# GLA decay differences as masked products on TensorE, moved gate stores and another issue plan in a hybrid SSD / GLA / RWKV-7 layer stack

## The chip, the cores and the metric

One core of a Trainium2 chip runs the whole program in a single launch. TensorE (PE) multiplies, with its weight loads listed apart as PEld; VectorE (DVE), ScalarE (ACT) and GpSimd (POOL) work element by element; SyncE (SP) issues most DMAs. The metric is the device time of one execution in microseconds, the median of several runs. The PE's clock has two levels, 1.2 and 2.4 GHz; the profile gives the share granted.

## The reference

Two layers (`DEPTH` 2) run over 128 context tokens and 256 latent tokens of width 1024. Each layer has a SwiGLU block, a token mixer of three scan branches (Mamba-2 SSD, GLA, RWKV-7, each forward and backward) and a second SwiGLU block. The change touches the GLA branch, which is, with chunks of C = 64 tokens:

```
lg = log_sigmoid(lr @ gk_w[d] + gk_b[d]) / 16
bc = cumsum(lg, within a chunk)
diff = bc[:, :, :, None] - bc[:, :, None, :]
decay = exp(where(causal, diff, -inf))
A = einsum('bnthk,bnshk,bntshk->bnhts', q, k, decay)
o_intra = einsum('bnhts,bnshv->bnthv', A, v)
q_dec = q * exp(bc);  k_dec = k * exp(last - bc)
S_{n+1} = exp(last) * S_n + k_dec^T v;  o = o_intra + q_dec @ S_n
```

There are 4 heads of 64 key and 128 value channels, and both directions are summed before an RMS norm, a gate and an output product.

## The kernel before

**Layout.** Activations stand with channels on the 128 partitions and all T = 384 tokens (6 chunks of 64) in the free dimension. The four GLA heads are two pairs (`hp` 0 and 1), each filling 128 partitions. Dense products are split in high and low fp32r parts: three products each, weights `wh` and `wl` made by ACT (`wh`) and DVE (`wl`) from a loaded tile `wraw`.

**The mixer's order.** The mixer first projects, and puts aside in DRAM, what the branches need; the last of this are the gates of three branches (`gates`, L1083 and on): a dense product in `psd`, a tanh on ACT into one of two staging tiles `sa`, and a store issued by SP. After the RWKV scan, `rwkv_out` of its second half and `gla_decays` (L1733) run together, with the last gate projections (`mhh`, `mhl`) as dense work between. Then `scans` (L811) runs the GLA lanes, the SSD lanes and the RWKV branch's output product (`ob` with `w_rw_o`, 96 dense products) together, and at the end the output products of GLA and SSD and the common output projection.

**What sets the order.** All lanes are Python generators. `pace` calls them in turn; while no lane is due, it issues single dense products. A lane says when it is due by the model `Clock` (L105): each instruction is put on its engine at an estimated time (`place`), and `yield` hands back when its operands are estimated to be there. So a change of the model's costs or rules moves instructions. Each engine then runs its own list in order and waits by semaphores. Because mixer instructions pass through the wrapper `Timed`, nearly all of them carry line L275 in the profile; the tile names tell them apart.

**GLA decays.** `gla_decays` forms for each pair and direction the gate `log_sigmoid` (tiles `gde` on ACT, `gdm` on DVE, table loads between exponential and logarithm), and its running sum within chunks by a scan on DVE: tile `b`, one for each pair and direction.

**GLA levels.** `gla_levels` (L1834) never forms the 64 x 64 x 64 decay. It cuts a chunk in six levels of halves; at each, with `b` of the middle token m, q takes exp(b_t - b_m) and k takes exp(b_m - b_s). For a pair and level, DVE takes two differences and POOL two (`gD<-b`), ACT one exponential of 768 columns (`gD<-gD`), DVE multiplies the half for q and POOL the half for k (`gD<-gD,glqk`), PE forms 12 products of 64 x 64, and DVE takes the level's entries into `A` by a masked copy (`gA`, COPY_PREDICATED). The operands of one level are made ahead.

**GLA states and output.** `gla_states` (L1777) makes exp(b) (`qe`) and exp(last - b) (`ke`) by DVE and ACT, q and k times these (`qd` on POOL, `ke` on DVE), and carries the states (`gS`). `gla_output` adds all products, then takes the norm (`gn`) and the gate (`go`, with `ggs`). The second pair's states wait for the first pair's output. The SSD stages beside it use `sR`, `sE`, `sD`, `sct`, `sx`.

Of the kernel before, what the change touches and what calls it, by code (L numbers as in the profile page):

```python
# [92 lines left out]

def split_evenly(n, parts, i):

    return n * (i + 1) // parts - n * i // parts if i < parts else 0
# [15 lines left out]
class Clock:  # L112
# [9 lines left out]

    LAG = dict(tensor=196, scalar=135, vector=128, gpsimd=75)
    LAG_TO = dict(tensor=50, gpsimd=30)

    def __init__(self, nc):
        self.nc = nc
        self.done = 0.0
# [12 lines left out]
    def place(self, engine, t, cost):  # L141
# [157 lines left out]
class GlaPair:  # L299


    def __init__(self):
        self.vt = self.A = None
        self.qd, self.states, self.done = {}, {}, False
# [33 lines left out]
class Kernel:  # L338
# [415 lines left out]
    def mixer_(self, l, nxt):  # L754
# [7 lines left out]
        with ExitStack() as st:  # L762
# [4 lines left out]
            with pool("mh") as mh, pool("stg") as self.stg, pool("rwp") as rp:  # L767
# [25 lines left out]
                decays = {}  # L793
# [17 lines left out]
    def scans(self, l, gp, sp, obp, decays, gin, sin, j):  # L811

        I = self.I
        go, lanes, pairs = self.gla(l, gp, decays, *gin[1:])
# [269 lines left out]
    def gates(self, l, b):  # L1084
# [616 lines left out]
    def gla(self, l, gp, b, q, k, v):  # L1701

        nc = self.nc
        o = gp.tile([128, 4, T], F32, name="go")
# [8 lines left out]
        def states(d):  # L1713
            for hp in range(2):
                p = P[hp]
                if d == 0:
                    p.vt = yield from self.gla_values(gp, v[:, 2 * hp:2 * hp + 2, :])
                yield from wait(lambda: p.vt is not None and (hp == 0 or P[0].done))
                yield from self.gla_states(l, gp, hp, d, q[:, hp, :], k[:, hp, :], b[hp, d], p)
# [4 lines left out]
        def levels():  # L1724
            for hp in range(2):
                P[hp].A = yield from self.gla_levels(gp, q[:, hp, :], k[:, hp, :], b[hp, 0], b[hp, 1])
                P[hp].gs = gp.tile([128, 2, T], F32, tag="gD", bufs=3, name="ggs")
# [5 lines left out]
    def gla_decays(self, l, gp, tp, b):  # L1733
        nc = self.nc
        gk = tp.tile([128, 2, 256], F32, name="gk")
        nc.gpsimd.memset(gk[64:96], 0.0)
# [3 lines left out]
        for hp in range(2):  # L1740
            em = []
            for d in range(2):
                bias = self.pa[l][:, A_GKB + 2 * d + hp:A_GKB + 2 * d + hp + 1]
                ps = self.psm()[:, :T]
                nc.tensor.matmul(ps, gk[64:96, d, 128 * hp:128 * hp + 128], self.misc[64:96, :], start=True, stop=True)
                e = tp.tile([128, T], F32, tag="te", bufs=2, name="gde")
# [474 lines left out]
```

## Time and profile before

| | us |
|---|---|
| median of 3 runs | 2452.38 |
| lowest and highest run | 2447.63, 2454.55 |
| profiled execution | 2450.24 |
| its span | 2448.2 |
| PE busy | 2308.2 |
| DVE busy | 1760.1 |
| ACT busy | 1104.5 |
| POOL busy | 510.1 |

The profile comes from one execution. Its page gives busy times and groups of equal instructions, and the trace behind it answers questions on single instructions, on what an engine waited for, and on stretches of the span. A group's row reads: line, engine, operation, written tile <- read tiles, shapes, count | busy time of all, mean ns of one | idle time before them and what ended it. The scan part of the first layer lies at about 742 to 906 us of the span, that of the second at about 1930 to 2097.

### The profile page before, as it was taken

To read this page: it belongs to the slowest core of one execution; us is meant where nothing else is said; L and a number is where in the kernel's file an instruction comes from. 1 tells how busy PE (TensorE), PEld (TensorE's weight loads), DVE (VectorE), ACT (ScalarE), POOL (GpSimd) and SP (SyncE) were. 2 spreads that over 40 slices of the span, in tenths; PEclk is the share of its full clock that TensorE was granted. 3 is DMA by queue.
4 is the path that set the end of the run, shared out by engine and by line. 5 is a ranking of instruction groups with operands and counts; after the bars stand their busy time and mean duration, and the time that the engine had idled before them with its cause. 6 is when DMAs were issued, how large, how long until landed. Compare 5 with 4: busy or idle time off the path is not lost. (4 is left out here: it accounts for less than half of the span.)

```text
span 2448.2 us, 48785 instructions
## 1 busy us (share of the span) xinstructions
PE 2308.2 (94%) x19825; PEld 2132.0 (87%) x19825; DVE 1760.1 (72%) x3152; ACT 1104.5 (45%) x2009; POOL 510.1 (21%) x582
## 2 busy tenths in 40 slices
PE   6999899899999879999999999989999987899998
PEld 4999897888877669999999999878888766899998
DVE  3968769776658987878486877995767597785433
ACT  3533346354435455543345334743544544463322
POOL 3100024212215641100120001441212275120000
PEclk7999999999999999999999999989999998999999
DMA  9766554334425226567465766423443431554432
GB/s 305 234 206 208 175 157 109 90 94 130 115 63 156 68 84 209 170 195 214 132 189 170 226 207 170 134 77 103 109 110 102 125 103 31 177 181 131 128 118 81
DMA packets 501663, 354.14 MB, mean 145 GB/s; under 512 B 40035, under 2 KB 479985, under 8 KB 500927
## 3 DMA queue, kind: packets, MB, share of 16 engines
q1 hardware_dynamic: 496288, 337.44, 46.9%
q0 software_dynamic: 3680, 6.18, 1.2%
q10 hardware_dynamic: 1471, 7.41, 0.8%
q8 instruction: 155, 2.54, 0.4%
q14 instruction: 69, 0.57, 0.1%
HBM read 326.59 MB, written 24.38 MB: 143 GB/s over the span
## 5 line engine op out<-in xcount | busy, mean ns | idle before, releaser
L649 ACT CAST wh<-wraw 128x1024 fp32r<-128x1024 f32 (+2 forms) x296 | 280.1, 956 | 585.7 <-issue 332.5
L650 DVE TENSOR_TENSOR wl<-wraw,wh 128x1024 fp32r<-128x1024 f32 (+2 forms) x296 | 330.8, 1125 | 220.6 <-ACT wh L649 220.3
L662 PE MATMUL psm<-xh,wl 128*128 128x384 f32 (+1 forms) x896 | 304.3, 340 | 5.8 <-DVE wl L650 5.8
L660 PE MATMUL psm<-xh,wh 128*128 128x384 f32 (+1 forms) x896 | 306.0, 342 | 0.6 <-DVE xh L608 0.6
L661 PE MATMUL psm<-xl,wh 128*128 128x384 f32 (+1 forms) x896 | 304.0, 339 | 0.0
L275 PE MATMUL psd<-mhl,wh 128*128 128x384 f32 x848 | 298.6, 352 | 2.6 <-DVE mhl L275 2.6
L275 PE MATMUL psd<-mhh,wh 128*128 128x384 f32 x848 | 295.2, 349 | 5.8 <-DVE sb L275 3.4
L275 DVE TENSOR_TENSOR wl<-wraw,wh 128x512 fp32r<-128x512 f32 x324 | 236.4, 742 | 85.4 <-ACT wh L275 78.7
L275 PE MATMUL psd<-mhh,wl 128*128 128x384 f32 x848 | 297.6, 351 | 0.0
L275 ACT CAST wh<-wraw 128x512 fp32r<-128x512 f32 x324 | 190.8, 614 | 174.3 <-PE psd L275 119.3
L536 DVE SCALAR_TENSOR_TENSOR aacc<-wada,cs,aacc 128x1024 f32<-128x1024 f32 x210 | 260.8, 1279 | 6.0 <-DMA wada<-in_w_ada_dram 5.6
L662 PE MATMUL psd<-gh,wl 128*128 128x384 f32 x704 | 237.1, 337 | 7.8 <-DVE wl L650 7.8
L660 PE MATMUL psd<-gh,wh 128*128 128x384 f32 x704 | 237.0, 337 | 0.0
L661 PE MATMUL psd<-gl,wh 128*128 128x384 f32 x704 | 236.5, 336 | 0.0
L621 POOL TENSOR_TENSOR acc<-acc,sq 128x384 f32<-128x384 f32 x24 | 28.9, 1205 | 718.6 <-ACT sq L619 709.2
L275 PEld LDWEIGHTS psd<-mhl,wh 128*128 128x128 f32 x848 | 162.6, 192 | 16.6 <-issue 8.1
L662 PEld LDWEIGHTS psm<-xh,wl 128*128 128x128 f32 x896 | 169.2, 189 | 8.1 <-DVE wl L650 7.9
L275 PEld LDWEIGHTS psd<-mhh,wh 128*128 128x128 f32 x848 | 162.7, 192 | 13.6 <-issue 5.8
L660 PEld LDWEIGHTS psm<-xh,wh 128*128 128x128 f32 x896 | 169.3, 189 | 6.0 <-issue 4.5
L660 PE MATMUL psm<-gh,wh 128*128 128x384 f32 x512 | 171.8, 336 | 0.0
L662 PE MATMUL psm<-gh,wl 128*128 128x384 f32 x512 | 171.1, 334 | 0.0
L661 PE MATMUL psm<-gl,wh 128*128 128x384 f32 x512 | 171.0, 334 | 0.0
(453 smaller groups left out, 4897.7 us busy)
## 6 DMA issues: line engine op xcount, KB each, us to landing
wada<-in_w_ada_dram SPq DMA_DIRECT2D x144, 512.0 KB, 4.8
wraw<-in_w_in_dram SPq DMA_DIRECT2D x112, 512.0 KB, 3.9
wraw<-in_ffn_gate_dram SPq DMA_DIRECT2D x88, 512.0 KB, 4.0
wraw<-in_ffn_up_dram SPq DMA_DIRECT2D x88, 512.0 KB, 4.7
wraw<-in_ffn_down_dram SPq DMA_DIRECT2D x64, 512.0 KB, 4.1
wraw<-in_ffn_down_dram SPq DMA_DIRECT2D x32, 384.0 KB, 4.6
gate<-sa SPq DMA_DIRECT2D x48, 192.0 KB, 2.3
gate<-gate SPq DMA_DIRECT2D x48, 192.0 KB, 2.5
```

Source lines behind the costliest of these rows:

```text
L275: r = f(*a, **k)
L536: nc.vector.scalar_tensor_tensor(out=acc[:, c], in0=w, scalar=x, in1=acc[:, c], op0=ALU.mult, op1=ALU.add)
L621: (nc.vector if k == KD - 1 else nc.gpsimd).tensor_tensor(out=self.acc, in0=self.acc, in1=sq, op=ALU.add)
L649: nc.scalar.copy(out=h[:, x], in_=r[:, x])
L650: nc.vector.tensor_sub(out=lo[:, x], in0=r[:, x], in1=h[:, x])
L660: nc.tensor.matmul(ps, wh, xh, start=first, stop=False)
L661: nc.tensor.matmul(ps, wh, xl, start=False, stop=False)
L662: nc.tensor.matmul(ps, wl, xh, start=False, stop=last)
```

## The change

Five things change together.

- `gla_decays` makes the gates with tokens on the partitions (12 products of 64 x 256 in place of 4 of 128 x 384, the bias from a loaded tile `gkb`), keeps the logarithms themselves, split in fp32r parts `lgh` and `lgl`, and makes no running sum.
- Every sum of logarithms that a level or a state needs is a product on PE with a column block of a 0/1 table `gsum` (128 x 1024, a new input built by `gla_sums`, loaded by POOL in each layer): `gla_sum` issues four products of 256 columns, and ACT takes the exponential straight from PSUM. This replaces the differences of DVE and POOL, `qe` and `ke` (now one tile `gE`).
- `gla_levels` goes through 9 stages for a pair (2 levels by 2 chunks each) in place of 6, with up to three operand tiles made ahead; a stage has one multiplication of 512 columns on DVE and one on POOL, 8 products of 64 x 64, and two masked copies of 128 columns.
- The stores of the last three gates of branch 0 are issued by POOL instead of SP.
- The model clock, during `scans`, puts an instruction in the first gap of its engine that holds it, with DVE, POOL and ACT costs taken 1.25, 1.3 and 1.1 times as long; before, it came behind all others of its engine. The output's gate tile `ggs` and the scratch of the norm get other places, and one SSD tile has three buffers for four.

```
@@ Clock @@
+    SLOWER = dict(vector=1.25, gpsimd=1.3, scalar=1.1)
...
-        if engine in ('vector', 'scalar', 'gpsimd'):
+        if self.gaps:
+            cost *= self.SLOWER.get(engine, 1.0)
+        elif engine in ('vector', 'scalar', 'gpsimd'):
@@ gates @@
-            self.nc.sync.dma_start(out=dst[i], in_=g)
+            (self.nc.gpsimd if b == 0 and i >= KD - 3 else self.nc.sync).dma_start(out=dst[i], in_=g)
@@ gla_sum, gla_inter: new @@
+        ps = self.psm()
+        for c in range(2):
+            for n, g in enumerate(b.parts):
+                nc.tensor.matmul(ps[:, 256 * c:256 * c + 256], g[:, 2 * j + c, 128 * hp:128 * hp + 128], b.sums[:, x:x + 256], start=(n == 0), stop=(n == 1))
+        nc.scalar.activation(out=out, in_=ps.rearrange("p (c s t) -> p c s t", c=2, s=4), func=AF.Exp, scale=1.0 / 16)
...
+        for j in range(3):
+            self.gla_sum(b, hp, j, 768, E[:, 2 * j:2 * j + 2])
...
+            nc.vector.tensor_mul(out=p.E[:, :, d, 1], in0=p.E[:, :, d, 1], in1=k)
...
+            nc.gpsimd.tensor_mul(out=p.E[:, :, d, 0], in0=p.E[:, :, d, 0], in1=q)
@@ gla_levels @@
-            nc.vector.tensor_tensor(out=DQ[:, :, 1], in0=f4[:, :, 1], in1=mf, op=ALU.subtract)
-            nc.vector.tensor_tensor(out=DQ[:, :, 0], in0=b4[:, :, 0], in1=mb, op=ALU.subtract)
-            nc.gpsimd.tensor_tensor(out=DK[:, :, 0], in0=mf, in1=f4[:, :, 0], op=ALU.subtract)
-            nc.gpsimd.tensor_tensor(out=DK[:, :, 1], in0=mb, in1=b4[:, :, 1], op=ALU.subtract)
-            nc.scalar.activation(out=DD, in_=DD, func=AF.Exp, scale=1.0 / 16)
-            nc.vector.tensor_mul(out=DD[:, 0], in0=DD[:, 0], in1=q)
-            nc.gpsimd.tensor_mul(out=DD[:, 1], in0=DD[:, 1], in1=k)
+            E = gp.tile([128, 2, 4, 64], F32, tag="gD", bufs=4, name="gD")
+            self.gla_sum(b, hp, j, 128 * lev, E)
+            E = E.rearrange("p c (l x) t -> p x c l t", l=2)
+            for i, eng in enumerate((nc.vector, nc.gpsimd)):
+                eng.tensor_mul(out=E[:, i], in0=E[:, i], in1=qk[i][:, 2 * j:2 * j + 2].unsqueeze(2).to_broadcast([128, 2, 2, 64]))
...
+            while len(nxt) < 3 and n + len(nxt) < len(stages):
+                nxt.append(operands(*stages[n + len(nxt)]))
```

How the lists of the engines move is shown at three places of the first layer. (In the changed kernel the wrapper's line is L300.)

POOL, from the end of the RWKV scan into the levels, before (`out_dram<-S` is the last RWKV state, `gk` the gate weights, `ro` the RWKV output, `dcol` and `ssi` are SSD's):

```order
L275 DMA out_dram<-S 128x2x64 x2
L275 MEMSET sC 128x768
L275 MEMSET gk 32x512
L275 DMA gk<-in_gla_gk_w_dram 16x256 x2
L275 TENSOR_TENSOR ro<-ro,kp 128x384 x2
L275 DMA dcol<-in_ssd_D_dram 64x4x1 x4
L275 DMA ssi<-in_state_ssd_dram 128x4x64 x2
L275 CAST smk<-kt 128x128 x3
```

and in the changed kernel:

```order
L300 DMA out_dram<-S 128x2x64 x2
L300 MEMSET sC 128x768
L300 DMA gsum<-in_sums_dram 128x1024
L300 MEMSET gk 64x512
L300 DMA gkb<-in_gla_gk_b_dram 64x256
L300 DMA gk<-in_gla_gk_w_dram 16x256 x2
L300 DMA gkb<-in_gla_gk_b_dram 64x256
L300 DMA gate_3181<-sa 128x384
L300 TENSOR_TENSOR ro<-ro,kp 128x384 x2
L300 DMA gate_3182<-sa 128x384
L300 DMA gate_3183<-sa 128x384
L300 DMA dcol<-in_ssd_D_dram 64x4x1 x4
```

The table load and a bias load stand ahead of the gate weights, and one gate store ahead of the `ro` product.

DVE, in the first pair's levels, before:

```order
L275 TENSOR_TENSOR gD<-b_8324 128x24x8
L275 TENSOR_TENSOR gD<-b_8328 128x24x8
L275 COPY_PREDICATED gA<-kt,psm 128x384
L275 TENSOR_TENSOR gD<-b_8324 128x48x4
L275 TENSOR_TENSOR gD<-b_8328 128x48x4
L275 SCALAR_TENSOR_TENSOR merged<-gate,psd 128x384
L275 TENSOR_TENSOR gD<-gD,glqk 128x384
```

and in the changed kernel:

```order
L300 TENSOR_TENSOR gD<-gD,glqk 128x4x64
L300 SCALAR_TENSOR_TENSOR merged<-gate,psd 128x384
L300 SCALAR_TENSOR_TENSOR gS<-gS,gtot,psm 128x128 x2
L300 COPY_PREDICATED gA<-kt,psm 128x128
L300 COPY gS<-psm 128x128
L300 COPY_PREDICATED gA<-kt,psm 128x128 x3
L300 SCALAR_TENSOR_TENSOR merged<-gate,psd 128x384
```

The differences are gone, and masked copies of a third of the size stand in their place.

PE, in the first pair's levels of the changed kernel; before, a level was one row `psm<-gD 64x64 x12` between dense products:

```order
L300 MATMUL psm<-gD 64x64 x8
L300 MATMUL psm<-gsum,lgh 128x256
L300 MATMUL psm<-gsum,lgl 128x256
L300 MATMUL psm<-gsum,lgh 128x256
L300 MATMUL psm<-gsum,lgl 128x256
L300 MATMUL psd<-ob,wh 128x384
L300 MATMUL psd<-ob,wl 128x384
```

The four sum products of a later stage follow the level products of the present one.

## Rows read from the trace of the kernel before

**Rows 1.** The page's part 1: busy time, share of the span and instructions.

```profile
PE 2308.2 (94%) x19825; PEld 2132.0 (87%) x19825; DVE 1760.1 (72%) x3152; ACT 1104.5 (45%) x2009; POOL 510.1 (21%) x582
```

**Rows 2.** Busy time by stretch; first layer's three stretches, second layer's levels.

```profile
core 0: us, PE busy (x) PEld busy (x) DVE busy (x) ACT busy (x) POOL busy (x), PEclk, DMA share, GB/s
742.00:763.00 21.00, 21.00 (x96) 16.19 (x94) 18.07 (x31) 18.95 (x30) 9.29 (x14) 1.00 0.55 133
763.00:834.00 71.00, 57.36 (x763) 48.53 (x764) 66.31 (x110) 32.94 (x63) 46.84 (x51) 0.92 0.40 114
834.00:906.00 72.00, 57.49 (x513) 46.28 (x509) 60.01 (x111) 36.77 (x74) 35.51 (x32) 0.92 0.16 48
...
1951.50:2022.00 70.50, 54.97 (x758) 46.48 (x759) 65.55 (x108) 32.26 (x61) 46.46 (x51) 0.94 0.40 113
```

**Rows 3.** Groups of instructions by form, both layers: level, state and POOL steps.

```profile
L275 POOL TENSOR_TENSOR gD<-gD,glqk 128x384 f32<-128x384 f32 x24 | 31.5, 1316 | 23.0 <-ACT gD L275 23.0
L275 DVE TENSOR_TENSOR gD<-b 128x192 f32<-128x192 f32 x48 | 27.9, 620 | 0.0
L275 DVE TENSOR_TENSOR gD<-gD,glqk 128x384 f32<-128x384 f32 x24 | 23.6, 984 | 3.8 <-ACT gD L275 3.8
L275 DVE COPY_PREDICATED gA<-kt,psm 128x384 f32<-128x384 int32 x24 | 13.9, 581 | 0.5 <-PE psm L275 0.4
L275 DVE SCALAR_TENSOR_TENSOR gS<-gS,qe,psm 128x128 f32<-128x128 f32 x32 | 9.6, 340 | 7.7 <-PE psm L275 5.1 <-DMA gS<-in_state_gla_dram 2.6
L275 DVE TENSOR_TENSOR ke<-ke,glqk 128x384 f32<-128x384 f32 x8 | 8.2, 1026 | 0.0
L275 DVE TENSOR_TENSOR ke<-b 128x384 f32<-128x384 f32 x8 | 7.1, 903 | 0.0
```

**Rows 4.** Timeline of DVE, two multiplications: start us, us, instruction, [idle before].

```profile
777.35 1.35 DVE L275 TENSOR_TENSOR gD<-gD,glqk 128x384 f32<-128x384 f32 x1
800.36 0.54 DVE L275 TENSOR_TENSOR gD<-gD,glqk 128x384 f32<-128x384 f32 x1
```

**Rows 5.** Timeline of POOL at the first of these.

```profile
776.98 1.31 POOL L275 TENSOR_TENSOR gD<-gD,glqk 128x384 f32<-128x384 f32 x1
```

**Rows 6.** Timeline of PE: gate products, two dense starts, one after small products.

```profile
750.80 1.55 PE L275 MATMUL psm<-misc,gk 32*128 32x384 f32 x4
...
754.14 0.34 PE L275 MATMUL psd<-mhh,wl 128*128 128x384 f32 x1
754.32 0.34 PE L275 MATMUL psd<-mhh,wh 128*128 128x384 f32 x1
...
794.75 0.44 PE L275 MATMUL psd<-ob,wh 128*128 128x384 f32 x1
```

**Rows 7.** Groups of ACT by form: exponentials from SBUF and from PSUM.

```profile
L275 ACT ACTIVATE gD<-gD 128x768 f32<-128x768 f32 x24 | 20.3, 846 | 32.0 <-DVE gD L275 25.3 <-POOL gD L275 6.7
L275 ACT ACTIVATE sct<-psm 128x512 f32<-128x512 f32 x16 | 9.1, 597 | 2.4 <-PE psm L275 2.4
```

**Rows 8.** Waits from 763 to 834 us: total us, times, longest us.

```profile
ACT gD L275 <- DVE gD L275: 12.5, 6, 3.2
...
PE psm L275 <- POOL gD L275: 4.2, 3, 2.9
...
ACT L275 <- DMA gate<-sa: 3.9, 1, 3.9
...
PE psd L275 <- ACT sa L275: 2.4, 1, 2.4
```

**Rows 9.** Timeline of POOL: issue of the gate weights.

```profile
738.81 1.03 POOL L275 DMA_DIRECT2D gk<-in_gla_gk_w_dram  x2 [0.29 <-POOL gk L275]
```

**Rows 10.** Groups of DVE by form, both layers: SSD and norm steps.

```profile
L275 DVE SCALAR_TENSOR_TENSOR sD<-scb,dt,sD 128x128 f32<-128x128 f32 x48 | 27.7, 608 | 1.8 <-ACT sD L275 1.8
L275 DVE TENSOR_TENSOR sE<-sE,sD 128x512 f32<-128x512 f32 x12 | 10.1, 840 | 0.1
L275 DVE SCALAR_TENSOR_TENSOR gn<-gn 128x384 f32<-128x384 f32 x8 | 8.0, 998 | 0.1
```

More of the change, by code (lines that the diff above doesn't have):

```diff
@@ L1703, in gla @@
         nc = self.nc
+        vt = [gp.tile([128, T // 64, 128], F32, tag="gvt", bufs=2, name="gvt") for hp in range(2)]
         o = gp.tile([128, 4, T], F32, name="go")
@@ L1762, in gla_values @@
-    def gla_values(self, gp, v):
-        nc = self.nc
-        NC = T // 64
-        vt = gp.tile([128, NC, 128], F32, tag="gvt", bufs=2, name="gvt")
+            nc.gpsimd.dma_start(out=bias[HS[d]], in_=self.I['gla_gk_b'][l, d].unsqueeze(0).to_broadcast([64, 256]))
+        em = []
+        for j in range(3):
+            ps = self.psm()
+            for c in range(2):
+                x = 64 * (2 * j + c)
+                for d in range(2):
+                    nc.tensor.matmul(ps[HS[d], 256 * c:256 * c + 256], self.misc[64:128, x:x + 64], gk[64:128, d, :], start=True, stop=True)
+            e, m = (tp.tile([128, 2, 256], F32, tag=n, bufs=3, name=n) for n in ("gde", "gdm"))
+            nc.vector.tensor_tensor(out=m, in0=ps.rearrange("p (c k) -> p c k", c=2), in1=bias.unsqueeze(1).to_broadcast([128, 2, 256]), op=ALU.add)
+            nc.scalar.activation(out=e, in_=m, func=AF.Abs)
+            nc.scalar.activation(out=e, in_=e, func=AF.Exp, scale=-1.0)
+            em.append((e, m))
+            yield self.soon()
@@ new lines, in gla_inter @@
+    def gla_inter(self, gp, hp, q, k, b, p):
+        nc = self.nc
+        E = gp.tile([128, 6, 4, 64], F32, tag="gE", bufs=1, name="gE")
+        for j in range(3):
+            self.gla_sum(b, hp, j, 768, E[:, 2 * j:2 * j + 2])
+            yield self.soon()
+        p.tot = gp.tile([128, 6, 2], F32, tag="gtot", bufs=2, name="gtot")
+        for d in range(2):
+            nc.scalar.copy(out=p.tot[:, :, d], in_=E[:, :, 2 * d, 63 if d == 0 else 0])
+        p.E = E.rearrange("p c (d x) t -> p c d x t", d=2)
+        q, k = (x.rearrange("p (c t) -> p c t", t=64) for x in (q, k))
+        for d in range(2):
+            nc.vector.tensor_mul(out=p.E[:, :, d, 1], in0=p.E[:, :, d, 1], in1=k)
+        p.ready = self.ck.done
+        for d in range(2):
+            nc.gpsimd.tensor_mul(out=p.E[:, :, d, 0], in0=p.E[:, :, d, 0], in1=q)
@@ new lines, in mask @@
+        def mask(lev, n):
+            return self.k(K_GM + 64 * lev, 64).unsqueeze(1).to_broadcast([128, n, 64])
+        nc.vector.tensor_tensor(out=A, in0=ps[:, 0:T].rearrange("p (c t) -> p c t", c=NC), in1=mask(6, NC), op=ALU.mult)
+        for n, (lev, j) in enumerate(stages):
+            while len(nxt) < 3 and n + len(nxt) < len(stages):
+                nxt.append(operands(*stages[n + len(nxt)]))
+                yield 0
+            E, t = nxt.popleft()
+            yield t
+            ps = self.psm()[:, 0:256].rearrange("p (l c t) -> p l c t", l=2, c=2)
+            for i in range(2):
+                for c in range(2):
+                    for hs in HS:
+                        nc.tensor.matmul(ps[hs, i, c], E[hs, 1, c, i], E[hs, 0, c, i], start=True, stop=True)
+            for i in range(2):
+                nc.vector.copy_predicated(out=A[:, 2 * j:2 * j + 2], mask=mask(lev + i, 2).bitcast(mybir.dt.int32), data=ps[:, i])
@@ L2038, in front @@
                 nc.tensor.matmul(pc[:, 0:256], Bm[:, bs], Cm[:, :, bs], start=True, stop=True)
-                cbs[b] = [sp.tile([128, 2, 128], F32, tag="scb", bufs=4, name="scb") for d in range(2)]
+                cbs[b] = [sp.tile([128, 2, 128], F32, tag="scb", bufs=3, name="scb") for d in range(2)]
                 for x, off in zip(cbs[b], (K_LE, K_GE)):
```

146 lines of the change are left out of this document (66 added, 80 removed).

## The prediction

> **What bounds the kernel now.** I read the page's busy times first: PE is busy for 94% of the span and DVE for 72% [rows 1], so over the whole program TensorE sets the time. But the change touches only the token mixer's scan part, once in each of the two layers, and an average over the program says nothing about that place. So I cut the first layer's scan part into three stretches and read the busy times of each [rows 2]: the decays (742 to 763 us), where PE is busy for all of 21 us; the level products (763 to 834), where DVE is busy for 66.3 of 71 us and PE for 57.4; and the tail (834 to 906: the second pair's states and outputs, and the SSD stages), where DVE has 60.0 and PE 57.5 of 72. The second layer's level stretch reads alike, 65.6 of 70.5 [rows 2], so everything below is worked out for one layer and doubled. In the decays every instruction added to PE is paid in full. In the level stretch VectorE is the bound, with a little over 13 us of idle PE beside it. The reader should see there how the waits run in a ring: the exponential on ACT and the products on PE wait for VectorE's and POOL's halves of the same operand tile [rows 8].
>
> **Decays.** Before, four fp32 products of 384 columns make the gates; two of them take 1.55 us with the last one's tail, so 0.75 each and 3.0 in all [rows 6]. Now there are twelve of 256 columns: at two thirds of 0.75 they take 6.0 us one after the other, and half of it, 3.0, if the two directions, which write different halves of the partitions, run side by side. So 0 to +3.0; I take +1.0, nearer to the lower end, since the small products of other lines run in such pairs already. POOL now loads the 512 KB mask table and one bias half ahead of the gate weights, which were issued at 738.81 for a first product at 742.18 [rows 9]. That product waits in PE's queue with the dense products behind it, so a late landing would be paid by PE: 0 to +2.5. The order puts 12 more dense products, 2.1 us at 0.173 [rows 6], ahead of the first gate product, and I take 0. VectorE's scans and two half-steps go and three wider steps and two splits come; the stretch is PE's, so they cost nothing while PE has its 58 dense products to run. POOL's queue gets the three gate stores, the first of them ahead of the `ro` product of the RWKV output, so this product waits for ACT's `sa`; it was needed only by the branch weights' first product after the dense ones, which is cover of about 8 us by the order. That they left SP frees the loads behind them; what this is worth stands in the next part. Decays: **+1.0**, between -0.5 and +5.
>
> **Levels, VectorE's work.** Per layer and in busy time (half of each row's sum, which covers both layers) there go 13.9 us of differences, 11.8 of multiplications, 6.9 of masked copies, and for the first pair 3.8 of the `ke` steps [rows 3]. In come 18 multiplications of 512 columns and 36 masked copies of 128. A multiplication of 384 columns takes 0.54 us at 800.36 but 1.35 at 777.35, where POOL was multiplying too [rows 4, 5], and 0.984 on average [rows 3]. Taken in proportion to the columns that is 0.72 to 1.31 on average; I take 1.1, nearer to the upper end, because one exponential still releases VectorE's and POOL's halves together: 19.8 us. A masked copy of 128 columns lies between a third of 0.581 and 0.581; the nearest row of that size is the `gS` step, which also reads PSUM, at 0.340 [rows 3]. I take 0.33: 11.9 us. The `gE` products of the first pair add two of 384 columns at about 0.8: 1.6. The order also moves work over the stretch's end: the first pair's normalisation (four `gn`, two `go`, one `ob`, about 0.8 each by [rows 10]: 5.6) now stands ahead of the last masked copy, and four `sD` steps, one `sE` and one `sR` (2.4 and about 1.7, [rows 10]) behind it. Out 36.4 + 4.1 = 40.5, in 19.8 + 11.9 + 1.6 + 5.6 = 38.9: **VectorE's work falls by 1.6 us only**. The many small copies give back much of what the differences cost.
>
> **Levels, the waits.** VectorE idles for 4.7 of the 71 us [rows 2]. At the start ACT waits 3.9 us for the landing of a gate store and PE 2.4 us for ACT behind it [rows 8]; SP had issued that store late. With the stores on POOL the wait for landing should go, and of VectorE's idle time perhaps 2 us with it. PE gets 84 products of 256 columns here (72 of the levels, 12 of the first pair's `gE`). A dense product of 384 columns starts every 0.173 us (two starts 0.18 apart, [rows 6]); in proportion 0.115, and not above 0.173. I take 0.12: 10.1 us, and 1.2 more for 18 groups of small products in place of 12, each change of shape costing about 0.1 on the way back ([rows 6], 0.44 against 0.34). PE then has 57.4 + 11.3 = 68.7, which no longer leaves it free, though part of the 57.4 ran at a granted clock of 0.92 [rows 2], that is with some of it at 1.2 GHz, and the denser stream should keep 2.4 GHz more. ACT is no issue: 12 exponentials of 768 columns at 0.846 become 24 of 512 at 0.597 from PSUM [rows 7], 14.3 us for 10.2, and the eight of `qe` and `ke` go. Work 1.6 less and idle 2 less, with 0.6 given back to PE: **-3.0**, between -10 and +6.
>
> **Tail.** The second pair's `ke` steps (3.8) and the first pair's norm (5.6) leave; two `gE` products (1.6) and the `sD`, `sE`, `sR` steps (4.1) come: VectorE has 3.7 us less of its 60.0. The stretch is not VectorE's alone, so I take **-3.5**, between 0 (the chain of SSD stages sets it) and -6.
>
> **The sum.** +1.0 - 3.0 - 3.5 = -5.5 for one layer, -11 for two. The profiled execution took 2450.24 us (span 2448.2 and 2.0 around it), so 2439.2; the median of the runs shown, 2452.38, lies 2.1 above it: **2441**.
>
> **A rule against the change.** The rows show VectorE's multiplication as long as POOL's beside it, 1.35 against 1.31 us [rows 4, 5]. The Trainium skill's page "SBUF — State Buffer", section "SBUF: two separate sides", says why: the two engines share a port pair as an exclusive lock for a whole instruction, and the loser blocks fully. The trace agrees in that pair of rows; taken at its word for every pair, it is the first rival.
>
> **Rivals.** (1) *The shared port.* Each of the 18 multiplications then lasts as long as POOL's, about 1.45 us (1.316 for 384 columns, [rows 3], and a little more for 512): 18 x 0.35 = 6.3 us more per layer, which makes the layer +0.8 and the program 2454. For it: in the rows the two halves do start together. Against it: half of the multiplications before ran unstretched, and POOL's own work falls, since its own differences, as many as VectorE's, go. (2) *PE becomes the bound.* The sum products stand in PE's order between the level products, and what waits for POOL and VectorE still waits: if the idle 13.6 us cannot be used, and the gate products run one after the other behind late weights, a layer costs decays +4, levels +3, tail -2: +5, program **2462, slower than before**. It decides as soon as PE's work in the level stretch exceeds about 68 us. For it: 68.7 above. Against it: the cold part of the 57.4. (3) *More than the sum.* If the longer look-ahead (three operand tiles made in advance, where there was one) takes the halves apart, multiplications cost 0.72 (-6.8) and the tail's waits shrink too: -16 per layer, 2420. For it: VectorE's queue no longer holds both halves of a difference behind POOL. Against it: both still follow one exponential.
>
> **How the numbers follow.** Forecast 0.42, shared port 0.23, PE bound 0.17, more than the sum 0.18. A measurement of this kernel tells about 0.3% from no change, 7.4 us: faster means below 2445, slower above 2460. The larger gain and most of the forecast's own spread make faster 0.54; the shared port and the forecast's upper edge make same 0.25; the PE bound and a little of the port's spread make slower 0.21. A range with a tenth left out at each end reaches from the middle of the larger gain, 2420, to the PE bound, 2462.
>
> **What would show it.** In the profile of the changed kernel: the mean of VectorE's 512-column multiplications (1.1 taken; 0.72 and 1.45 are the rivals) and of the masked copies (0.33); starts of the sum products 0.12 us apart; no ACT wait for a gate store at the start of the levels; PE idle and clock in the level stretch; the decays 1 us longer, the levels 68 and the tail 68.5 us. I am wrong if the stretch lengths hardly move while VectorE's share falls (another wait took over), or if the decays grow by more than 3 us (late gate weights).

## The result and the profile of the changed kernel

The changed kernel takes **2469.9 us** (median; 2464.5 to 2471.3), the kernel before 2451.0 in the same comparison: a ratio of **1.0084** (95% interval 1.0070 to 1.0097), slower by 18.9 us. The forecast was 2441, its range ended at 2462: wrong in sign and outside the range. The profiled execution of the changed kernel took 2464.5 (span 2462.5), 14.3 more than the span before.

The page's busy times, to be read against [rows 1]:

```profile
PE 2328.4 (95%) x20049; PEld 2149.8 (87%) x20049; DVE 1733.7 (70%) x3150; ACT 1108.8 (45%) x2025; POOL 480.7 (20%) x558
```

The work went as the change says: VectorE has 26 us less, POOL 29 less, TensorE 20 more. Busy time by stretch, to be read against [rows 2]: the first layer's decays, levels and tail, then the second layer's levels.

```profile
core 0: us, PE busy (x) PEld busy (x) DVE busy (x) ACT busy (x) POOL busy (x), PEclk, DMA share, GB/s
742.50:761.45 18.95, 18.91 (x98) 14.64 (x99) 14.14 (x26) 16.52 (x23) 3.27 (x4) 1.00 0.37 128
761.45:834.91 73.46, 65.96 (x830) 56.60 (x829) 56.11 (x114) 37.84 (x72) 33.37 (x42) 0.95 0.45 111
834.91:912.42 77.51, 61.11 (x534) 48.78 (x535) 58.83 (x105) 33.43 (x73) 38.86 (x35) 0.91 0.14 39
1959.00:2032.53 73.53, 66.40 (x831) 56.98 (x829) 50.84 (x114) 37.88 (x72) 33.33 (x42) 0.95 0.44 111
```

In the levels VectorE fell from 66.3 of 71 to 56.1 of 73.5 (50.8 in the second layer), and the stretch grew all the same. TensorE went from 57.4 to 66.0. The tail, with VectorE at 58.8, grew from 71 to 77.5.

The groups of the new steps, to be read against [rows 3]:

```profile
L300 POOL TENSOR_TENSOR gD<-gD,glqk 128x256 f32<-128x256 f32 x36 | 30.9, 865 | 58.7 <-ACT gD L300 57.3 <-DVE gA L300 1.1
L300 PE MATMUL psm<-gsum,lgh 128*128 128x256 f32 x96 | 29.2, 329 | 2.0 <-DVE gA L300 2.0
L300 DVE TENSOR_TENSOR gD<-gD,glqk 128x256 f32<-128x256 f32 x36 | 21.9, 607 | 4.6 <-ACT gD L300 4.5
L300 DVE COPY_PREDICATED gA<-kt,psm 128x128 f32<-128x128 int32 x72 | 21.4, 298 | 10.5 <-PE psm L300 9.8
```

One thing jumps out: a stage's multiplication has 256 columns on each engine, not 512 as the change was described and the prediction took it. The tile holds 512, half for q and half for k. The start times of the sum products on TensorE are 0.12 us apart, as the prediction took them:

```profile
761.46 0.29 PE L300 MATMUL psm<-gsum,lgh 128*128 128x256 f32 x1
761.59 0.28 PE L300 MATMUL psm<-gsum,lgl 128*128 128x256 f32 x1
761.71 0.29 PE L300 MATMUL psm<-gsum,lgh 128*128 128x256 f32 x1
```

**What ends the scan part.** VectorE's step `sE` of the SSD stages comes six times in a layer. Here are the first and last of them (timeline of VectorE), with the `sD` steps and the last masked copy beside the first, before:

```profile
830.79 1.39 DVE L275 SCALAR_TENSOR_TENSOR sD<-scb,dt,sD 128x128 f32<-128x128 f32 x2
...
832.57 0.67 DVE L275 TENSOR_TENSOR sE<-sE,sD 128x512 f32<-128x512 f32 x1
833.17 0.58 DVE L275 COPY_PREDICATED gA<-kt,psm 128x384 f32<-128x384 int32 x1
...
894.05 0.68 DVE L275 TENSOR_TENSOR sE<-sE,sD 128x512 f32<-128x512 f32 x1
```

and in the changed kernel:

```profile
842.01 1.47 DVE L300 TENSOR_TENSOR sE<-sE,sD 128x512 f32<-128x512 f32 x1
...
901.95 0.67 DVE L300 TENSOR_TENSOR sE<-sE,sD 128x512 f32<-128x512 f32 x1
```

In both kernels the SSD output (`ob<-sx` on ACT) starts 10.5 us after the last: at 904.52 and 912.42. From the first `sE` to the last it is 61.5 us before and 59.9 now. Counted from the end of the decays (the start of their last dense product, `psd<-mhh`, at 763.0 and 761.3), the first comes at 69.6 before and at 80.7 now, the last at 131.1 and 140.7. So the row of six steps starts later, and is as long as before. VectorE's order offers a reason: before, one `sE` and four `sD` ran ahead of the last masked copy (833.17); now all of them stand behind it. No run moves these steps alone, so that this is the cause is argued and not shown. The timeline of VectorE in the changed kernel:

```profile
834.62 0.29 DVE L300 COPY_PREDICATED gA<-kt,psm 128x128 f32<-128x128 int32 x1
...
836.08 3.69 DVE L300 SCALAR_TENSOR_TENSOR sD<-scb,dt,sD 128x128 f32<-128x128 f32 x3
```

The trace also tells which engines the end waited for. Followed back from the start of the SSD output, at each step to what released it or else to the instruction before it on its engine (as the page does for the last instruction), the time after the decays consists in the kernel before of about 48 us on TensorE and 47 on VectorE in the first layer, 46 and 59 in the second. In the changed kernel it is about 69 and 48, and 78 and 51, with 11 us for a load (`dcol`, below) in each layer. The end waited for both engines, and TensorE's share is the one that grew.

One remark on the change as described ahead: the rule of the model clock is switched on in the first scans and never off, so it plans the second layer's mixer too.

### The profile page after: what moved, and what is told of

Read it like the earlier page. It is cut to its first block, busy times and chain, and to the rows that moved or that the text cites. A ratio compares the mean times of both kernels' runs of the same rounds, so it can differ in the third digit from the quotient of the medians.

```text
span 2462.5 us, 49213 instructions
## 1 busy us (share of the span) xinstructions
PE 2328.4 (95%) x20049; PEld 2149.8 (87%) x20049; DVE 1733.7 (70%) x3150; ACT 1108.8 (45%) x2025; POOL 480.7 (20%) x558
## 5 line engine op out<-in xcount | busy, mean ns | idle before, releaser
L300 PE MATMUL psd<-mhh,wh 128*128 128x384 f32 x848 | 293.3, 347 | 6.0 <-DVE sb L300 3.4
L300 PE MATMUL psd<-mhl,wh 128*128 128x384 f32 x848 | 296.5, 350 | 2.5 <-DVE mhl L300 2.5
L300 DVE TENSOR_TENSOR wl<-wraw,wh 128x512 fp32r<-128x512 f32 x324 | 242.2, 759 | 76.4 <-ACT wh L300 69.5
L300 PE MATMUL psd<-mhh,wl 128*128 128x384 f32 x848 | 294.7, 348 | 0.0
L300 ACT CAST wh<-wraw 128x512 fp32r<-128x512 f32 x324 | 190.3, 615 | 172.1 <-PE psd L300 109.1
L300 PEld LDWEIGHTS psd<-mhl,wh 128*128 128x128 f32 x848 | 161.1, 190 | 14.1 <-issue 5.8
L300 PEld LDWEIGHTS psd<-mhh,wh 128*128 128x128 f32 x848 | 161.1, 190 | 13.3 <-issue 5.8
L690 PEld LDWEIGHTS psm<-xl,wh 128*128 128x128 f32 x896 | 169.4, 189 | 0.3
```

Of the source, the lines that this page charges most:

```text
L300: r = f(*a, **k)
L690: nc.tensor.matmul(ps, wh, xl, start=False, stop=False)
```

## The experiments

Two measures stand side by side. The ratio of a kernel to the kernel before, with its interval; and the **scan part**: from the issue of the last RWKV state's store to the first product of the mixed output (`mgh`), in the profiled execution, first and second layer. The second is needed because the stretch between the two scan parts varies too. TensorE's order through the second layer's RWKV scan is the same, but for swaps of neighbouring 32 x 32 products, in the kernels compared for it (before, changed, e2, e3, e6, e10, e11, e13), and yet its time differs by up to 12 us. For the kernel before, then for e11 and e10, from the first mixed output to the second layer's state store:

```profile
923.85:1924.05 1000.20, 978.04 (x8317) 924.16 (x8317) 735.52 (x1296) 451.29 (x812) 145.99 (x165) 0.99 0.53 155
```

```profile
928.37:1937.94 1009.57, 982.06 (x8317) 927.39 (x8317) 735.21 (x1296) 451.39 (x812) 145.66 (x165) 0.98 0.53 154
```

```profile
920.06:1917.44 997.38, 974.15 (x8317) 920.21 (x8317) 735.20 (x1296) 451.41 (x812) 145.74 (x165) 0.99 0.53 156
```

The same 8317 products, 4 us more or less busy at a granted clock of 0.98 or 0.99, and some idle time. Why is not shown: each kernel has one profiled execution, and executions of the kernel before alone range from 2438.4 to 2454.9 us beside e9 to e12.

How far an edit leaves the order alone can be read from the traces. Of VectorE's steps in the first layer's scan part, all 285 of e13 stand in the changed kernel's order, 284 of e4, 275 of e2 and 270 of e6. In the order of the kernel before stand 265 of 286 in e11, 243 of 286 in e9, 219 of 286 in e3, and 187 of 262 in e12. So e9, e3 and e12 are other plans as well as other work.

| kernel | median us | ratio (interval) | scan part, layers 1, 2 | first, last `sE` after decays |
|---|---|---|---|---|
| before (2448.3 to 2451.0 beside the others) | 2451.0 | 1 | 188.1, 190.8 | 69.6, 131.1 |
| changed | 2469.9 | 1.0084 (1.0070 to 1.0097) | 199.0, 201.3 | 80.7, 140.7 |
| e1 changed, old rule | 2472.4 | 1.0098 (1.0084 to 1.0113) | 202.1, 201.9 | 83.9, 145.7 |
| e2 changed, high sums only | 2469.2 | 1.0085 (1.0071 to 1.0100) | 194.4, 198.6 | 77.0, 135.4 |
| e3 before, new rule | 2443.8 | 0.9971 (0.9958 to 0.9983) | 185.1, 186.5 | 71.0, 127.8 |
| e4 changed, stores on SP | 2461.5 | 1.0056 (1.0044 to 1.0068) | 195.5, 197.9 | 77.4, 137.2 |
| e5 masked products alone | 2456.9 | 1.0033 (1.0019 to 1.0046) | 195.7, 192.9 | 78.2, 138.7 |
| e6 changed, sums doubled | 2483.1 | 1.0136 (1.0119 to 1.0154) | 206.3, 206.1 | 84.0, 146.7 |
| e7 changed, SSD first | 2511.9 | 1.0253 (1.0234 to 1.0272) | 218.4, 219.5 | 34.8, 101.0 |
| e8 changed, one ahead | 2461.7 | 1.0046 (1.0029 to 1.0062) | 197.6, 195.0 | 79.0, 138.0 |
| e9 before, stores on POOL | 2459.4 | 1.0043 (1.0027 to 1.0058) | 196.8, 196.6 | 70.3, 139.6 |
| e10 one ahead, stores on SP | 2445.6 | 0.9987 (0.9974 to 1.0000) | 187.5, 190.2 | 72.6, 129.7 |
| e11 before, 84 products | 2466.5 | 1.0076 (1.0061 to 1.0090) | 194.9, 195.6 | 75.3, 137.7 |
| e12 before, no VectorE differences | 2456.7 | 1.0037 (1.0023 to 1.0051) | 194.8, 198.1 | 70.1, 135.2 |
| e13 changed, dcol on SP | 2466.4 | 1.0068 (1.0052 to 1.0084) | 197.6, 197.6 | 78.0, 139.0 |
| e14 e10, high sums only | 2461.6 | 1.0056 (1.0043 to 1.0068) | 190.6, 194.6 | 69.4, 132.6 |
| e15 e10, both halves on DVE | 2455.8 | 1.0026 (1.0016 to 1.0035) | 193.5, 190.4 | 73.2, 134.4 |
| e16 e10, old rule | 2469.0 | 1.0083 (1.0059 to 1.0108) | 199.1, 200.0 | 78.5, 142.9 |

Theory A: TensorE's work in the scan part is paid, so the sum products are the loss. Theory B: the loss is the issue plan, which starts the SSD stages late.

### The cost side alone: TensorE products added, taken out, doubled

**e11** adds products to the kernel before.

```
 ps = self.psm()
+for i in range(6):
+    self.ck.nc.tensor.matmul(ps[:, 0:256], self.ob_now[0][:, 0, 0:128], self.ob_now[0][:, 1, 0:256], start=True, stop=True)
 for c in range(NC):
```

> The kernel before with 84 additional TensorE products of 256 columns in each layer's levels (six ahead of each level's products, into the same PSUM tile, written over by them; the model clock does not count them), 0.118 us apart: 9.9 us of TensorE a layer, and nothing else. It measures the cost side of the change alone. If VectorE bounds the levels and TensorE's 13.6 idle us there take the products (the prediction's reading), 4 us more at most in all, 2454 or less. If TensorE's work is paid wherever it stands in the scan part (theory A), 60 to 100% of 19.8 us: 2460 to 2470.

Measured: 17.5 us more, 0.88 of the 19.8, as Theory A expected. But only 11.5 of it lies in the scan parts (6.7 and 4.8); the rest is in the stretch between them shown above, and unexplained. Whole scan parts of e11:

```profile
733.49:928.37 194.88, 169.41 (x1581) 143.03 (x1580) 162.27 (x286) 99.43 (x184) 94.69 (x103) 0.95 0.35 99
1937.94:2133.50 195.56, 171.34 (x1582) 144.64 (x1580) 164.99 (x286) 99.31 (x184) 94.91 (x104) 0.94 0.35 102
```

and of the kernel before:

```profile
735.71:923.85 188.14, 159.50 (x1498) 133.76 (x1496) 164.41 (x286) 98.76 (x184) 97.80 (x103) 0.94 0.36 103
1924.05:2114.81 190.76, 160.50 (x1497) 134.67 (x1496) 164.20 (x286) 98.84 (x184) 97.69 (x104) 0.93 0.36 104
```

TensorE is busy 9.9 us more in the first layer, and its idle time falls from 28.6 to 25.5 only. In this order most of TensorE's idle time is waiting for something, not room for products.

**e2** takes the products of the low part out of the changed kernel, **e6** issues each twice.

```
-for n, g in enumerate(b.parts): matmul(o, g, sums, start=(n == 0), stop=(n == 1))
+matmul(o, h, sums, start=True, stop=True)
+self.ck.count('tensor', 'matmul', o, (r, sums), {})
```

```
+for g in b.parts:
+    self.ck.nc.tensor.matmul(o, g, sums, start=True, stop=True)
 for n, g in enumerate(b.parts): matmul(o, g, sums, start=(n == 0), stop=(n == 1))
```

> The changed kernel without the products of the low part (lgl) of the logarithms: 48 of the 96 sum products of a layer are left out, so the decays are those of the high part alone; the model clock still counts them, so that all other instructions keep their order on every engine. Theory A (TensorE bound): 48 x 0.118 = 5.7 us less in each layer, 2457 to 2461 in all. Theory B (issue plan): the order is unchanged, so 2466 to 2470.

> The changed kernel with each sum product issued twice: 96 more products of 256 columns in each layer, 0.118 us apart, 11.3 us of TensorE a layer, written over by the regular ones; the model clock does not count them, so the issue order stays nearly the same. Theory A (TensorE is the bound of the level stretch): nearly all is paid, 18 to 23 us more than the changed kernel, 2488 or more, and the level stretch grows from 73.6 to 83 or more. Theory B (the late SSD stages set the end, and TensorE has room): under 8 us more, 2478 or less.

e6 takes 13.2 us more than the changed kernel, 12.1 of it in the scan parts: half of the 22.7 that were added, between the ranges of both theories. e2 gains 7.2 us in the scan parts, of 11.3 taken out, and nothing in the time, where Theory B had it: its stretch between them took 1006.2 us, the changed kernel's 999.2. So with nearly the same order, TensorE's work in the scan part is paid there by some 0.53 to 0.64 of it (12.1 of 22.7, 11.5 of 19.8, 7.2 of 11.3). For the 22.7 us of sum products in the change that is an estimated 12 to 15 us. Of the whole time the share is less sure: 0.88 in e11, 0.58 in e6, none in e2.

### The gain side alone: VectorE relieved

**e12** leaves VectorE's differences out of the kernel before.

```
-nc.vector.tensor_tensor(out=DQ[:, :, 1], in0=f4[:, :, 1], in1=mf, op=ALU.subtract)
-nc.vector.tensor_tensor(out=DQ[:, :, 0], in0=b4[:, :, 0], in1=mb, op=ALU.subtract)
...
-nc.scalar.activation(out=DD, in_=DD, func=AF.Exp, scale=1.0 / 16)
+nc.scalar.activation(out=DD[:, 0], in_=bf, func=AF.Exp, scale=1.0 / 16)
+nc.scalar.activation(out=DD[:, 1], in_=DD[:, 1], func=AF.Exp, scale=1.0 / 16)
```

> The kernel before without VectorE's differences in the levels: 24 instructions of 0.62 us in each layer are left out, and the exponential of q's half reads the running sum itself (two exponentials of 384 columns for one of 768), so the level decays are not the reference's. It measures the gain side of the change alone: 14.9 us less VectorE work a layer. If VectorE is the bound of the level stretch (the prediction's reading), most of it is gained: 20 us or more in all, 2429 or less. If other chains are as long as VectorE's work, under 10 us: 2440 or more.

Measured: 7.7 us *more*. Its first layer's levels and tail:

```profile
759.54:826.22 66.68, 57.35 (x766) 47.22 (x765) 57.74 (x88) 38.28 (x78) 44.63 (x51) 0.95 0.44 127
826.22:905.51 79.29, 61.07 (x503) 49.26 (x503) 59.87 (x106) 31.62 (x67) 36.76 (x33) 0.85 0.13 38
```

The levels are 4.1 us shorter (70.8 before), the tail 8.5 longer (70.8 before), at a granted clock of 0.85. The first `sE` comes when it came (70.1 for 69.6), the third at 107.1 for 97.2. So with 24 steps of 0.62 us gone from VectorE, 4.1 us came out of the levels, and the scan part as a whole got longer. This speaks against VectorE alone as the bound, but does not settle it: the planner also made another order (75 of VectorE's other 262 steps moved), and what the differences are worth in an unchanged order is not shown.

### The issue plan: lane order, look-ahead, rule

> The changed kernel with the SSD lanes ahead of the GLA lanes in the list that is called in turn; nothing else. Theory B (the late SSD stages set the tail): the first SSD product comes some 30 us after the end of the decays, as before the change (28.2), and not 65.3; the tail falls from 77.5 back to about 71, the time by 8 to 14 us, 2456 to 2462. Theory A (TensorE bound): the work is only moved, 2467 to 2473.

```
-self.pace(lanes + more + [after_gla()], 10000)
+self.pace(more + lanes + [after_gla()], 10000)
```

The SSD steps came first (34.8), and the scan parts took 19 and 18 us longer: GLA's second pair came last, its last output cast 157 us after the decays (125 in the changed kernel). Theory B in this simple form falls: putting SSD first only changes which row of steps is late.

> The changed kernel with one operand tile of the levels made ahead, where there are up to three in the change with the present one. If the look-ahead is what lets the GLA lane pass the SSD lanes (theory B), the SSD products start earlier and the time falls to 2460 to 2466. If the look-ahead hides the way from sum product over exponential and multiplication to the level products, the levels grow by 5 us a layer or more: 2478 or more. Theory A says 2468 to 2474.

```
-while len(nxt) < 3 and n + len(nxt) < len(stages):
+while len(nxt) < 2 and n + len(nxt) < len(stages):
```

8.2 us less, in the range that stood for Theory B: a shorter look-ahead is better here. But the SSD steps hardly start earlier. The levels are 3 us longer, the tail 5 and 8 us shorter; the row of `sE` starts 1.7 us sooner and ends 2.7 us sooner.

**e3** adds the rule to the kernel before, **e1** takes it from the changed one (the flag `gaps` and the factors `SLOWER`).

> The kernel before with one part of the change added: the model clock's new rule (first gap that holds it; DVE, POOL, ACT costs 1.25, 1.3, 1.1 times) from the first scans on. Theory A (TensorE bound): the rule alone does little, 2448 to 2454. Theory B (issue plan): the rule itself costs, 2458 or more.

> The changed kernel with one part undone: the model clock keeps the old rule during the scans (an instruction comes behind all others of its engine, costs of DVE, POOL and ACT as they were). Changed kernel 2469.9 us, kernel before 2451.0, so 18.9 us are to be explained. Theory A (TensorE bound: the 96 sum products of a layer, about 0.118 us apart, 11.3 us a layer, fall on a stretch in which TensorE had no usable room): the rule matters little, 2467 to 2473. Theory B (issue plan: the new rule lets the GLA lane go ahead and puts the SSD stages, whose first products moved from 791 to 826 us, into the tail): most of the loss goes, 2452 to 2460, and the first SSD state products return to within 10 us of 791.

The rule by itself makes the kernel before faster by 5.2 us: the last `sE` comes at 127.8 for 131.1. In the changed kernel its removal changes the time within the intervals, where Theory B expected most of the loss to go. Neither theory expected the gain in e3, and its order is another one. e3 is faster than both kernels of this case.

### The gate stores

```
-(self.nc.gpsimd if b == 0 and i >= KD - 3 else self.nc.sync).dma_start(out=dst[i], in_=g)
+self.nc.sync.dma_start(out=dst[i], in_=g)
```

> The changed kernel with one part undone: the last three gate stores of branch 0 issued by SP again. Prediction's step: the start of the levels waited 3.9 us on ACT for the landing of a gate store and 2.4 us on TensorE behind it, and the move to POOL should save some 2 us a layer: 2472 to 2476 if that holds here; 2468 to 2471 if the wait no longer reaches the end; under 2467 if the stores on POOL hold up what stands behind them on its queue (the ro product, at 755.4 us for 753.7 before).

> The kernel before with one part of the change added: the last three gate stores of branch 0 issued by POOL. The prediction's step: ACT's 3.9 us and TensorE's 2.4 us wait at the start of the levels go, some 2 us a layer gained, 2445. By the runs on the changed kernel (stores on POOL cost 8 us there with the new rule and 16 with the old one), it costs: 2457 or more, with the decays longer, because POOL's queue stands at the stores until ACT has written sa, and the ro product and loads behind them wait.

e4 is the edit shown; e9 is its reverse in the kernel before. Stores back on SP gain 8.4 us (6.8 in the scan parts) with the order kept; stores on POOL cost the kernel before 10.3, in another order. The trace of the changed kernel shows how; first POOL's queue:

```profile
764.53 0.54 POOL L300 DMA_DIRECT2D gate<-sa  x1 [3.79 <-ACT sa L300]
765.06 2.46 POOL L300 DMA_DIRECT2D dcol<-in_ssd_D_dram  x4
```

The four small loads of `dcol` stand behind the third store, which waits for ACT's `sa`. Before, they were issued at 755.74. VectorE then waits for their landing, and the masked copies and `merged` steps stand behind that in its queue; TensorE waits for `merged` (timelines of VectorE, first and second layer, and of TensorE, first layer). In the first layer VectorE's own wait is short only because a split ahead of it was held for 6.01 us (last section); in the second, without such a hold, it waits 6.20 us:

```profile
778.39 0.16 DVE L300 TENSOR_TENSOR dcol<-dcol 128x4 f32<-128x4 f32 x1 [0.85 <-DMA dcol<-in_ssd_D_dram]
...
1975.65 0.16 DVE L300 TENSOR_TENSOR dcol<-dcol 128x4 f32<-128x4 f32 x1 [6.20 <-DMA dcol<-in_ssd_D_dram]
```

```profile
780.20 1.01 PE L300 MATMUL psd<-ob,wh 128*128 128x384 f32 x2 [5.52 <-DVE merged L300]
```

In e9 it is much the same chain: VectorE waits 4.77 us for `dcol`, the differences stand behind it, then ACT's exponential and POOL's half behind those, and TensorE waits 8.25 us:

```profile
772.76 0.16 DVE L275 TENSOR_TENSOR dcol<-dcol 128x4 f32<-128x4 f32 x1 [4.77 <-DMA dcol<-in_ssd_D_dram]
```

```profile
777.60 0.69 PE L275 MATMUL psm<-gD 64*64 64x64 f32 x8 [8.25 <-POOL gD L275]
```

**e13** moves `dcol` alone.

```
-nc.gpsimd.dma_start(out=dcol[64 * a:64 * a + 64, d, :], in_=src.to_broadcast([64, 4]))
+nc.sync.dma_start(out=dcol[64 * a:64 * a + 64, d, :], in_=src.to_broadcast([64, 4]))
```

> The changed kernel with the four small loads of dcol issued by SP; the gate stores stay on POOL, VectorE's and ACT's order is unchanged. If the stores cost because dcol stands behind them in POOL's queue: VectorE's wait for dcol (0.85 and 6.2 us in the two layers, up to 778.4) and TensorE's 5.5 and 4.9 us wait behind VectorE go, the levels fall from 73.6 to about 70, the time by about 8 us to 2460 to 2464, as with the stores on SP. If the ro product or the state loads behind the stores are the cause: 2467 to 2472.

This settles it by half: the levels fell to 70.9 and 70.6 (73.6 and 73.7 in the changed kernel), as expected, and TensorE's wait behind `merged` to 3.1 us. But SP issued the loads late as well: VectorE still waited 4.3 and 4.9 us for them. The time is 3.5 us lower, within the intervals and between the two expected ranges, since the tail got longer by up to 2 us. That `dcol` carries the whole price of the stores is thus not shown.

### What is left when stores and look-ahead are set back

> The changed kernel with two things set back: one operand tile made ahead, and the gate stores on SP. Each alone brought about 8 us. If they add up, 2453 or 2454, a few us above the kernel before; if both mend the same wait, 2460 to 2462.

2445.6 us: 24 us less than the changed kernel, more than the two single gains together (16.6), and 3 us under the kernel before, at the edge of the interval. First layer's scan part of e10, and its row of `sE`:

```profile
732.58:920.06 187.48, 167.26 (x1609) 142.78 (x1608) 148.13 (x285) 100.32 (x192) 85.47 (x88) 0.97 0.38 108
```

```profile
832.35 0.68 DVE L300 TENSOR_TENSOR sE<-sE,sD 128x512 f32<-128x512 f32 x1
...
889.42 0.68 DVE L300 TENSOR_TENSOR sE<-sE,sD 128x512 f32<-128x512 f32 x1
```

TensorE has 7.8 us more work than before, and its idle time is 20.2 for 28.6 us: in this order the products do fit.

> The changed kernel with two parts undone, the new rule of the model clock and the gate stores on POOL: what is left is the GLA part on sum products and masks, with its new tile places. If the parts add up, by the runs so far (new rule on the kernel before: -5.2 us; stores back on SP: -8; new rule off in the changed kernel: +2.5) this part alone costs about 15 us more than the kernel before, some 2464. If the parts need each other (the new plan was made for the masked products), 2470 or more. If the loss was only in the two small parts, 2452 or less.

> The changed kernel with one operand tile ahead and the stores on SP (2445.6 as it stands), and without the low part of the logarithms: 48 sum products of each layer and the three splits that make the low part are left out, so the decays are those of the high part alone. Theory A (TensorE's work in the scan part is paid, by 0.94 of 19.8 us in the kernel before): 48 x 0.118 x 2 = 11.3 us less TensorE work, 2434 to 2437, which would be under both kernels. If the products lie in idle time here: 2443 to 2447.

> The changed kernel with one operand tile ahead and the stores on SP (2445.6), and POOL's multiplications of the levels (18 a layer of 0.87 us) issued by VectorE instead. VectorE gets 18 x 0.41 = 7.4 us more a layer and loses what its instructions are held up beside POOL (splits of 1.19 us for 0.68, multiplications of 0.58 for 0.41: some 10 us a layer in the changed kernel). If these holds reach the end: 2438 or less. If VectorE's time does not matter (theory A): 2442 to 2449. If VectorE becomes the bound of the levels: 2455 or more.

> The changed kernel with one operand tile ahead, the gate stores on SP and the old rule of the model clock: the masked products are the only part of the change that is left. What ends the scan part in all runs so far is the row of six SSD steps sE, the last one some 11 us before the SSD output: 131.1 us after the decays before the change, 140.7 in the changed kernel, 129.7 with one stage ahead and stores on SP, 127.8 in the kernel before with the new rule. If the old rule suits the masked products better, as it did with the stores on SP and three stages ahead (1.0033 for 1.0056): 2438 to 2442. If the rule brings with one stage ahead what it brought in the kernel before: 2449 to 2453.

```
-for i, eng in enumerate((nc.vector, nc.gpsimd)):
+for i, eng in enumerate((nc.vector, nc.vector)):
```

Added parts do not explain these runs: e5, e14 and e16 lie outside every range that stood for them, and e15 in the one for VectorE as the bound of the levels (2455 or more). e5 (three ahead, old rule, SP) takes 8 us more than the kernel before. e16 differs from e5 by the look-ahead alone, and there the shorter one *costs* 12 us. e14 has 11.3 us less TensorE work than e10 and takes 16 us more: its order is another one: the first `sE` comes 3.2 us earlier and the last 2.9 later, the scan parts are 3.1 and 4.4 longer, and the stretch between them took 1005.8 us for e10's 997.4. e15 moves POOL's multiplications to VectorE and takes 10 us more than e10: 6.0 and 0.2 in the scan parts, 7.3 in the stretch between them. So more work on VectorE may cost there; with 22 of VectorE's other 285 steps moved as well, it is not shown. Edits of the lanes often make another plan, and one plan can differ from the next by more than the edit's own work. With the same rule and the stores on SP, the masked products never beat the old levels: 2445.6 against e3's 2443.8 with the new rule, 2456.9 and 2469.0 against 2451.0 with the old one.

## Why the prediction was wrong, step by step

- **The bound of the level stretch.** "VectorE is the bound, with a little over 13 us of idle PE beside it" is the step that failed: it let the sum products overlap with VectorE's work at almost no charge. e11 put 19.8 us of products into that idle time and the program took 17.5 us more, 11.5 of it in the scan parts; the change itself took 10 to 15 us of busy time from VectorE in each layer's levels, and the levels grew by 2.9 and 2.8. A busy share of 66.3 in 71 said that VectorE was full, not that the end waited for it alone: the steps followed back from the end lie on TensorE about as long as on VectorE in the first layer before (48 and 47 us), and much longer after (69 and 48). The prediction had named the sign itself: VectorE's share falls (66.3 of 71 to 56.1 of 73.5) and the stretch is not shorter, so another wait took over. The last steps of that path are SSD steps: in all kernels but e7 the SSD output begins 8 to 13 us after the sixth `sE`.
- **The levels, work.** The multiplications were mis-sized: 512 columns at 1.1 us taken, 256 at 0.607 found. That is 10.9 us a layer for 19.8. The masked copies were right (0.298 for 0.33). So VectorE lost far more work than the 1.6 us of the sum; its busy time in the levels fell by 10 to 15 us. Sized rightly, the step would have forecast a larger gain still; for the stretch -3.0 was taken, and +2.9 and +2.8 came.
- **The sum products.** Price and count were right (0.12 us each). Only 0.6 us a layer was charged for them beside VectorE's relief; by the three runs on TensorE's work they cost an estimated 12 to 15 us in the two layers.
- **The tail.** -3.5 was taken, +6.7 and +6.5 came. The prediction saw in the order that four `sD` and an `sE` move behind the last masked copy, and booked them as work that leaves one stretch and enters the other. They are the start of a row, and in the changed kernel the row starts 11 us later and ends 10 us later. But a start in time is not enough: with the first `sE` at 69 to 71 us, the last came at 127.8 (e3), 131.1 (before), 132.6 (e14), 135.2 (e12) and 139.6 (e9). What holds up the later steps stays open.
- **The stores.** They were costed at nothing, with the `ro` product as the one to look at, and 2 us of gain. The loads behind them in POOL's queue were not followed to their user. The stores cost 8.4 us in the changed kernel (e4), 10.3 in the kernel before (e9, in another order). The 3.9 us wait of ACT for a store's landing did go from the first layer's levels.
- **The decays.** +1.0 was taken; +1.2 and +0.6 came. The number was right by luck: the +1.0 stood for the gate products, and nothing for late gate weights. The products take 3.4 us in both kernels (first layer: 0.91, 0.91 and 1.55 us before; 1.25, 1.08 and 1.08 now), and TensorE waited 1.10 us for the weights:

```profile
742.54 1.25 PE L300 MATMUL psm<-gk,misc 64*64 64x256 f32 x8 [1.10 <-DMA gk<-in_gla_gk_w_dram]
```

- **The rivals.** The second one (TensorE becomes the bound, 2462) had the right sign, and its levels, +3, are what came. Its tail, -2, was as wrong as the forecast's, and its condition was not met: TensorE is busy for 66.0 us in the levels, not 68. The third counted on the look-ahead; e8 and e10 say that it costs with the new rule (e5 against e16 says that it gains with the old one). The first, the shared port, shows at other instructions: a split was held for 6.01 us beside POOL (last section), while the multiplications averaged 0.607. The page "SBUF — State Buffer" of the Trainium skill, section "SBUF: two separate sides", says that one engine has the shared port pair for a whole instruction and the other blocks fully; that split, which did not end before POOL's run of instructions did, fits this, though it lost for longer than any one of them.

What is shown: two costs in the scan parts, added TensorE work (e11, e6, e2) and the stores on POOL (e4). That VectorE's relief gains nothing is not shown: in the change it came together with both costs, and in e12 with another order. What stays open: why the stretch between the scan parts differs, why one plan's row of `sE` is 57 us long (e10) and another's 64 (e16), and how much of the loss each part is, since the parts do not add up: the same step on or off gives 8 to 16 us for the stores on POOL, -12 to +16 for the longer look-ahead and -23 to +5 for the new rule, by what else is set.

## What to carry to other kernels

A full engine is the bound only if the end waits for it: before costing a relief, follow the chain that ends the stretch, here a row of equal steps whose first and last start can be read from the trace, and ask what each of its steps waits for and whether the change starts the row sooner or later. Work moved behind the last step of something else can be a start that is moved, not a sum that stays. A DMA that is put on another queue is costed by everything issued behind it, each followed to its user; and where a planner sets the order, a part's worth measured in one plan is not its worth in the next.

## What the runs showed of the hardware

VectorE was held much longer beside POOL than by one instruction. In the first layer of the changed kernel a split of 512 columns, 0.68 us when alone, took 6.01 (timeline of VectorE):

```profile
771.52 6.01 DVE L300 TENSOR_TENSOR wl<-wraw,wh 128x512 fp32r<-128x512 f32 x1
```

while POOL worked without a gap (timeline of POOL):

```profile
771.96 1.41 POOL L300 TENSOR_TENSOR gD<-gD,glqk 128x256 f32<-128x256 f32 x2
773.34 1.97 POOL L300 TENSOR_TENSOR gE<-gE,glqk 128x384 f32<-128x384 f32 x2
775.27 0.71 POOL L300 TENSOR_TENSOR gD<-gD,glqk 128x256 f32<-128x256 f32 x1
775.96 1.03 POOL L300 TENSOR_TENSOR sR<-adl,kt 128x512 fp32r<-128x512 f32 x1
```

It ended within 0.6 us of POOL's last. The next step, `dcol`, would have had to wait until then anyway, as in the second layer, where the same place shows no such hold and VectorE waits 6.20 us. In e4, where `dcol` lands in time (0.35 us of waiting at most), a multiplication of `gE` was held for 5.88 us in the first layer and one of `gD` for 5.40 in the second. What such holds are worth at the end is not shown: e15 took POOL's multiplications away, but gave them to VectorE, and was slower than e10.
